# Loading k and v for two pairs of sequences at a time, 1 MB per transfer

## The chip, the cores and the metric

The kernel runs on one core of one Trainium2 chip. The metric is the device time of one execution in microseconds (us). Runs are called fast, or slow when they lie over 1.5% above the fastest run of the same kernel; on one core that label says nothing about why. Profiled times ("span") are a little shorter than the run's time: the span of 386.6 us belongs to a run of 388.32 us.

## The reference, cut to what matters

For each of 16 sequences of 2048 steps and 256 channels, two running sums are carried from step to step; `k`, `v` and the output are 33.6 MB each.

```python
for t in range(seq_len):
    ww = u + kk;       qq = max(pp, ww)            # output of step t
    output[b, t, :] = (e1 * aa + e2 * vv) / (e1 * bb + e2 + 1e-08)
    ww = pp - w + kk;  qq = max(ww, kk)            # state for step t + 1
    aa = e1 * aa + e2 * vv
    bb = e1 * bb + e2
    pp = qq
```

## The kernel before

Time is cut into a short head of 32 steps and 16 *chunks* of 126 steps. Within a chunk the steps lie on the partitions, so the sums over time are matmuls. A *pair* is four sequences of one chunk (two groups of two); four pairs make a chunk, and one pair is one *iteration* of the loop. The output of a pair is made 11 iterations after its input (`LAG`), because it needs the state of all earlier chunks first. Three things matter here.

**The loads.** Each iteration loads `k` and `v` of the pair three iterations ahead, 512 KB each, into one of four buffers. GpSimd issues them, and it also issues the stores of the output, in program order.

```python
AHEAD = 3
kpool = ctx.enter_context(tc.tile_pool(name="kpool", bufs=AHEAD + 1))   # vpool likewise
...
def load(n):
    kr = kpool.tile([128, 4, Dm], F32, tag="kr", name="kr")
    vr = vpool.tile([128, 4, Dm], F32, tag="vr", name="vr")
    ...
        for t, x in ((kr, k), (vr, v)):
            K(POOL.dma_start(out=t[0:r, :, :],
                           in_=x[4 * p:4 * p + 4, t0:t0 + r, :].rearrange("n t d -> t n d")))
```

**The state.** Once a chunk, its column sums `ts` leave the chip's PSUM by ScalarE and are sent by SyncE in six small transfers (`tsum`). VectorE and ScalarE make the new state `ab` from them. SyncE then sends `ab` in four 8 KB transfers into rows 126 and 127 of the tiles `ez`, from where the matmul `den` (128 rows: 126 steps and the state) takes it. Two of the four must be there before the first `den` of the chunk can start.

```python
def inject(c):
    ab = small.tile([128, 2, 64], BF16, tag="ab16", name="ab16")
    K(DVE.tensor_mul(ab, AB.pop(c)[:, :, 0, :], st.pop((c, "phi"))))
    for j in range(2):
        for h in range(2):
            K(SP.dma_start(out=EZ[1 + 2 * c + j][TC + h:TC + h + 1, 0:2, :, :].rearrange(...),
                           in_=ab[64 * j:64 * j + 64, h, :]))
```

**The loop.** The order below is the order on each engine. TensorE, VectorE, ScalarE and GpSimd each take their part of it strictly in turn.

```python
for n in range(NP + LAG + 1):
    ...
    if n + AHEAD < NP:
        load(n + AHEAD)
    small_work(n, "first")
    exps(n)                    # ez = exp(X), ScalarE
    sums(n - 1)                # tot, TensorE
    round_k(n + 1)             # km <- kr, VectorE: the first reader of k
    num(qp, 0); den(q); recip(q); mult(qp, 0); num(qp, 1)
    small_work(n, "pool")      # state_chain, inject
    times_v(n)
    mult(qp, 1); store(qp)
    logs(n + 1)                # X, TensorE
    cast_v(n + 1)              # vb <- vr, VectorE: the first reader of v
```

## Time and profile before

| | before |
|---|---|
| median of 3 runs | 385.43 us (382.28 to 395.25) |
| profiled span, mean granted TensorE clock | 386.6 us, 0.925 |
| busy: TensorE, VectorE, ScalarE, GpSimd | 71%, 78%, 73%, 44% |
| from issue to landing, medians: kr, vr, store | 7.7, 8.1, 6.4 us |
| chunk periods, 157 to 323 us | 18.7 and 22.0 to 23.8 us in turn, mean 20.8 |

The prediction below shows the page's lines and reads them.

The starts of the 66 `ez` activations give the length of every iteration. In the steady part of the kernel before (from 157 us on), three of the four iterations of a chunk take 5.2, 3.8 and 5.8 us (once 6.0). Only the fourth, in which `den` waits for the state, varies: 4.0 us in one chunk, 7.2 to 9.1 us in the next. In each, this is about 3 us and the stall of `den`. So the chunk is 14.8 + 3 + stall, and with the mean stall of 38.5 / 13 = 3.0 us this gives the measured 20.8 us.

The page is of a run that is called slow (388.32 against 382.28 us).

### The profile page before, as it was taken

The page shows a single profiled execution, that of the slowest core. Times are in us where ns is not written, and L with a number is a line of the kernel's source. Part 1 is how long each engine was busy: PE and PEld are TensorE (multiplying, and loading weights), DVE is VectorE, ACT ScalarE, POOL GpSimd, SP SyncE. Part 2 cuts the span into 40 slices and gives each one's busy share as a digit, 9 for nine tenths or more (in the row PEclk, how much of TensorE's full clock was granted, in tenths as well). Part 3 has the DMA queues.
Part 4 walks back from the last instruction along what each step waited for, and adds up shares of the span by engine and source line. Part 5 has one row for each costly group of instructions (what it writes and reads, how often), then busy time and mean ns, then how long its engine had stood idle before and what let it go on. Part 6 is the DMA issues. An engine that isn't in the chain of part 4 may idle for free.

```text
span 386.6 us, 4003 instructions
## 1 busy us (share of the span) xinstructions
PE 275.0 (71%) x1033; PEld 138.0 (36%) x1048; DVE 302.2 (78%) x595; ACT 283.4 (73%) x282; POOL 171.5 (44%) x252
## 2 busy tenths in 40 slices
PE   0276667969886883978598858878587939776771
PEld 0143333435443442434254424444343515322220
DVE  2867789898988885899879977899689967956441
ACT  1165577978897784989598976898698939875571
POOL 7663433554645251555455452546355523121221
PEclk9999989898999896999989998999899978987796
DMA  8499995899999897899989997999899999645454
GB/s 204 130 293 339 332 297 137 269 278 331 330 308 353 290 315 282 236 331 333 352 278 315 314 351 260 332 318 345 290 293 343 303 280 254 198 125 150 128 173 148
DMA packets 49718, 105.72 MB, mean 273 GB/s; under 512 B 24096, under 2 KB 25136, under 8 KB 49696
## 3 DMA queue, kind: packets, MB, share of 16 engines
q0 software_dynamic: 29136, 100.65, 79.3%
q1 hardware_dynamic: 19968, 4.30, 6.0%
q10 hardware_dynamic: 592, 0.52, 0.6%
q8 instruction: 8, 0.13, 0.1%
q14 instruction: 14, 0.11, 0.1%
HBM read 68.11 MB, written 33.55 MB: 263 GB/s over the span
## 4 chain that ended last, share of the span: by engine, by line
ACT 27%; DMA 26%; PE 20%; DVE 12%; issue 10%; POOL 2%; SPq 1%; POOLq 0%; ACTq 0%; DVEq 0%
DMA ez<-ab 17%; ACT ez L252 16%; DMA vr<-in_v_dram 9%; PE X L241 8%; ACT rd L402 5%; PE den L394 5%; PE num L412 4%; PE tot L299 3%; DVE rd L420 3%; ACT ts L309 2%; ACT ts L308 2%; DVE ez L268 2%; DVE vb L260 1%; ACT rd L403 1%; SPq L382 1%
## 5 line engine op out<-in xcount | busy, mean ns | idle before, releaser
L252 ACT ACTIVATE ez<-X 128x2048 bf16<-128x2048 f32 x66 | 122.1, 1850 | 24.8 <-PE X L241 24.7
L436 POOL DMA_DIRECT2D out_dram<-rd x64 | 55.6, 869 | 177.9 <-ACT rd L403 99.7
L420 DVE TENSOR_TENSOR rd<-num,rd 126x512 f32<-126x512 f32 (+1 forms) x131 | 89.8, 685 | 32.2 <-PE num L412 26.9
L268 DVE TENSOR_TENSOR ez<-ez,vb 126x2048 bf16<-126x2048 bf16 (+1 forms) x66 | 80.1, 1213 | 21.6 <-ACT ez L252 20.1
L402 ACT ACTIVATE rd<-den 126x1024 f32<-126x1024 f32 (+1 forms) x66 | 66.7, 1011 | 35.9 <-PE den L394 35.9
L403 ACT ACTIVATE rd<-rd 126x1024 f32<-126x1024 f32 (+1 forms) x66 | 69.4, 1051 | 2.1
L241 PE MATMUL X<-km,NLE 128*128 128x512 f32 x128 | 54.6, 510 | 20.0 <-ACT ez L252 16.6
L412 PE MATMUL num<-ez,LfN 128*128 128x512 bf16 x128 | 51.8, 405 | 23.3 <-DVE rd L420 22.5
L394 PE MATMUL den<-ez,Lf 128*128 128x512 bf16 x113 | 37.6, 404 | 38.5 <-DMA ez<-ab 38.5
L105 POOL DMA_DIRECT2D vr<-in_v_dram x64 | 49.9, 779 | 21.2 <-DVE vb L260 14.9
L105 POOL DMA_DIRECT2D kr<-in_k_dram x64 | 54.4, 851 | 1.4 <-DVE km L233 0.9
L412 PE MATMUL num<-ez,IdN 126*128 126x512 bf16 (+1 forms) x131 | 53.2, 406 | 0.0
L299 PE MATMUL tot<-ez,OHV 126*96 126x512 bf16 x128 | 50.2, 392 | 2.2 <-DVE ez L268 2.2
L299 PE MATMUL tot<-ez,OHE 128*96 128x512 bf16 x128 | 49.7, 388 | 1.1 <-ACT ez L252 1.0
L233 DVE CAST km<-kr 126x1024 fp32r<-126x1024 f32 (+1 forms) x66 | 46.5, 705 | 1.9 <-DMA kr<-in_k_dram 1.6
L260 DVE CAST vb<-vr 126x1024 bf16<-126x1024 f32 (+1 forms) x66 | 45.3, 687 | 0.0
L394 PE MATMUL den<-ez,Id 126*128 126x512 bf16 (+1 forms) x131 | 43.7, 417 | 2.0 <-issue 1.6
L241 PE MATMUL X<-km,NLZ 128*128 128x512 f32 x128 | 41.6, 407 | 0.0
L241 PEld LDWEIGHTS X<-km,NLE 128*128 128x128 f32 x128 | 24.3, 208 | 41.8 <-ACT ez L252 35.3
L394 PEld LDWEIGHTS <-Lf 128*128 128x128 bf16 x128 | 12.1, 101 | 58.2 <-DMA ez<-ab 32.5
L412 PEld LDWEIGHTS <-IdN 126*128 126x128 bf16 (+1 forms) x131 | 13.3, 102 | 51.4 <-issue 44.6
L339 ACT ACTIVATE g<-ex 128x256 f32<-128x256 f32 (+1 forms) x17 | 6.9, 408 | 29.2 <-DVE ex L332 26.9
(89 smaller groups left out, 213.4 us busy)
## 6 DMA issues: line engine op xcount, KB each, us to landing
out_dram<-rd POOLq DMA_DIRECT2D x64, 504.0 KB, 6.4
kr<-in_k_dram POOLq DMA_DIRECT2D x60, 512.0 KB, 7.7
vr<-in_v_dram POOLq DMA_DIRECT2D x60, 512.0 KB, 8.1
tsum<-ts SPq DMA_DIRECT2D x99, 32.0 KB, 5.9
kr<-in_k_dram POOLq DMA_DIRECT2D x4, 504.0 KB, 9.6
vr<-in_v_dram POOLq DMA_DIRECT2D x4, 504.0 KB, 10.9
ez<-ab SPq DMA_DIRECT2D x64, 8.0 KB, 6.9
kr<-in_k_dram SPq DMA_DIRECT2D x3, 128.0 KB, 3.7
```

The costliest lines, as they stand in the source:

```text
L105: K(POOL.dma_start(out=t[0:r, :, :], in_=x[4 * p:4 * p + 4, t0:t0 + r, :].rearrange("n t d -> t n d")))
L241: K(PE.matmul(X[:, q, i, :], m[0:kr, :], km[0:kr, i, :], start=True, stop=True))
L252: K(SC.activation(ez_of(n)[:, 0:4:2], X_of.pop(n)[:, :, 0:i, :], ACT.Exp))
L260: K(DVE.tensor_copy(vb[0:r, 0:i, :], vr_of.pop(n)[0:r, 0:i, :]))
L268: K(DVE.tensor_mul(ez[0:r, 1:4:2], ez[0:r, 0:4:2], vb[0:r, 0:i, :].unsqueeze(1).broadcast_to([r, 2, i, D])))
L299: K(PE.matmul(TOT[c], m[0:r, :], ez_of(n)[0:r, q, i, :], start=n == first_of(c) and i == 0 and q == 0, stop=n == last_of(c) and i == tiles ...
L394: K(PE.matmul(d[:, i, :], m[0:r, :], ez_of(n)[0:r, q, i, :], start=q == 0, stop=q == 2, skip_group_check=True))
L402: K(SC.activation(rd[0:r, 0:i, :], DEN.pop(n)[0:r, 0:i, :], ACT.Ln, scale=RS))
L403: K(SC.activation(rd[0:r, 0:i, :], rd[0:r, 0:i, :], ACT.Exp, scale=-1.0))
L412: K(PE.matmul(d, m[0:r, :], ez_of(n)[0:r, q, i, :], start=q == 1, stop=q == 3, skip_group_check=True))
L420: K(DVE.tensor_mul(RD[n][0:r, i, :], NUM.pop((n, i))[0:r, :], RD[n][0:r, i, :]))
L436: K(POOL.dma_start(out=out[4 * p:4 * p + 4, t0:t0 + TC, :].rearrange("n t d -> t n d"), in_=o[0:TC, :, :]))
```

## The change

The intent is to have half as many transfers of twice the size. The buffers of `k` and `v` hold two pairs, there are two of them instead of four of one pair (the same memory), and both loads are issued together at the end of every even iteration.

```diff
-    kpool = ctx.enter_context(tc.tile_pool(name="kpool", bufs=AHEAD + 1))
-    vpool = ctx.enter_context(tc.tile_pool(name="vpool", bufs=AHEAD + 1))
+    kpool = ctx.enter_context(tc.tile_pool(name="kpool", bufs=2))
+    vpool = ctx.enter_context(tc.tile_pool(name="vpool", bufs=2))
...
-    def load(n):
-        kr = kpool.tile([128, 4, Dm], F32, tag="kr", name="kr")
-        vr = vpool.tile([128, 4, Dm], F32, tag="vr", name="vr")
+    def load(G):
+        kr = kpool.tile([128, 8, Dm], F32, tag="kr", name="kr")
+        vr = vpool.tile([128, 8, Dm], F32, tag="vr", name="vr")
+        for n in (2 * G, 2 * G + 1):
+            i = 4 * (n % 2)
+            kr_of[n], vr_of[n] = kr[:, i:i + 4, :], vr[:, i:i + 4, :]
...
-                               in_=x[4 * p:4 * p + 4, t0:t0 + r, :].rearrange("n t d -> t n d")))
+                               in_=x[4 * p:4 * p + 8, t0:t0 + r, :].rearrange("n t d -> t n d")))
...
-        if n + AHEAD < NP:
-            load(n + AHEAD)
...
             cast_v(n + 1)
+        if n % 2 == 0 and n + 4 < NP:
+            load(n // 2 + 2)
```

More of the change, by code (lines that the diff above doesn't have):

```diff
@@ L44 @@
     NH = NG * GB
-    AHEAD = 3
     LAG = 11
@@ L83, in head_view @@
         return e - b, x[b:e, 0:T0, :].rearrange("n t d -> t n d")
-    def load(n):
-        kr = kpool.tile([128, 4, Dm], F32, tag="kr", name="kr")
-        vr = vpool.tile([128, 4, Dm], F32, tag="vr", name="vr")
-        kr_of[n], vr_of[n] = kr, vr
-        if is_head(n):
-            if n == 1:
-                K(DVE.memset(kr[64:96, 0:2, :], 0.0))
-                K(DVE.memset(vr[64:96, 0:2, :], 0.0))
-            for t, x, eng in ((kr, k, SP), (vr, v, SC)):
-                for g in range(NG):
-                    b = 6 * g + 4 * n
-                    e = min(b + 2 * tiles_of(n), B)
-                    if b < e:
-                        K(eng.dma_start(out=t[g * GB:(g + 1) * GB, 0:e - b, :],
-                                        in_=x[b:e, 0:T0, :].rearrange("n t d -> t n d")))
-        else:
-            c, p = pairs[n]
+    def load(G):
[4 more added lines that the diff above has]
+            kr_of[n], vr_of[n] = kr[:, i:i + 4, :], vr[:, i:i + 4, :]
+            if is_head(n):
+                if n == 1:
+                    K(DVE.memset(kr[64:96, i:i + 2, :], 0.0))
+                    K(DVE.memset(vr[64:96, i:i + 2, :], 0.0))
+                for t, x, eng in ((kr, k, SP), (vr, v, SC)):
+                    for g in range(NG):
+                        b = 6 * g + 4 * n
+                        e = min(b + 2 * tiles_of(n), B)
+                        if b < e:
+                            K(eng.dma_start(out=t[g * GB:(g + 1) * GB, i:i + e - b, :],
+                                            in_=x[b:e, 0:T0, :].rearrange("n t d -> t n d")))
+        if G:
+            c, p = pairs[2 * G]
             t0 = T0 + c * TC
@@ L113 @@
             tensor=x.tensor, offset=x.offset, ap=[[0, 1], [0, 4], list(x.ap[0])])))
-    for n in range(1, AHEAD):
-        load(n)
+    load(1)
     M1 = consts.tile([128, 128], F32, tag="M1", name="M1")
```

## The prediction

> **What bounds the kernel now.** I read the page first, then the waits, then the windows, then the timeline of GpSimd. Each pair of sequences (66 of them: 2 short head pairs, then 16 chunks of 4 pairs) is one iteration of a software-pipelined loop. No engine is full on the page, but the DMA row is:
>
> ```profile
> PE 275.0 (71%) x1033; PEld 138.0 (36%) x1048; DVE 302.2 (78%) x595; ACT 283.4 (73%) x282; POOL 171.5 (44%) x252
> ...
> DMA  8499995899999897899989997999899999645454
> ...
> q0 software_dynamic: 29136, 100.65, 79.3%
> q1 hardware_dynamic: 19968, 4.30, 6.0%
> ```
>
> The digits are tenths of the 16 DMA engines' time in 40 slices of 9.7 us: 9 from slice 3 to slice 34, with a few dips, then about 5 in the tail, where nothing is loaded. q0 holds the loads of k and v and the stores, q1 the small transfers that SyncE issues (`tsum` and `ez<-ab`). The windows view gives the middle, 100 to 345 us:
>
> ```profile
> core 0: us, PE busy (x) PEld busy (x) DVE busy (x) ACT busy (x) POOL busy (x), PEclk, DMA share, GB/s
> 100.00:345.00 245.00, 187.66 (x732) 96.05 (x742) 206.06 (x387) 198.38 (x200) 111.47 (x134) 0.94 0.93 298
> ```
>
> VectorE works 84% of it, ScalarE 81%, the DMA engines 93%. Yet the loads themselves are in time; what waits for DMA is something else, as the view of waits says:
>
> ```profile
> POOL out_dram L436 <- ACT rd L403: 99.7, 35, 7.7
> ...
> PE den L394 <- DMA ez<-ab: 38.5, 13, 6.2
> ...
> POOL vr L105 <- DVE vb L260: 14.9, 7, 3.1
> ...
> DVE km L233 <- DMA kr<-in_k_dram: 1.6, 3, 0.7
> ```
>
> Columns are total us, times, longest. VectorE waited 1.6 us for k. TensorE stood 38.5 us, 13 times, for `ez<-ab`, an 8 KB transfer (four per chunk) that carries the running state into the `den` matmul; it is also the largest item of the chain that ended last (17%). In the timeline those four leave SyncE from 181.06 us on, the first two, which `den` needs, landed at 190.8 and 191.4, and `den` had stood 4.3 us by then. In an idle machine the same transfer is quick: from 345 us on its median is 2.8 us to landing, from 60 to 345 us it is
>
> ```profile
> DMA to landing us min/median/max: 2.1/7.5/10.6
> ```
>
> The landing records show why. A small transfer lands right behind the bulk transfer issued before it: `tsum` issued at 26.35 us landed at 32.79, the load of k issued at 24.05 landed at 32.58. So its latency is the backlog of q0. Latency of `ez<-ab` is a measure of how far the DMA engines are behind, and the stall is how the DMA limit shows itself.
>
> Starts of successive `ts` activations give the chunk periods: 18.7, 22.0, 18.7, 22.9, 18.7, 22.6, 18.7, 23.8 us from 157 to 323 us, mean 20.8. In the 18.7 us chunks the stall is about 1 us and costs nothing (the four iterations take 5.2, 3.8, 5.8 and 4.0 us); in the others it is 4.3 to 5.7 us. So 18.7 us is the pace of the engines without the stall. The DMA's own need per chunk: 8 loads of 512 KB and 4 stores of 504 KB are 1,528 packets of 4 KB. In full stretches the trace has 85 to 90 of them a microsecond, so 17.0 to 18.0 us; `tsum` and `ez` traffic adds about 1 us. That is 18.0 to 19.0 us, level with 18.7. The rest, 20.8 - 18.7 = 2.1 us a chunk, is lost where the queue has nearly run dry and starts again: at 110 to 115, 131 to 135, 154 to 159, 195 to 199 us, once a chunk, packets fall to 40 to 60 a microsecond. It comes after a gap in which GpSimd, whose queue is in order, waits with a store and holds the loads behind it back:
>
> ```profile
> 186.91 0.84 POOL L436 DMA_DIRECT2D out_dram<-rd  x1 [1.35 <-ACT rd L403]
> 187.74 1.14 POOL L105 DMA_DIRECT2D kr<-in_k_dram  x1
> 188.87 0.75 POOL L105 DMA_DIRECT2D vr<-in_v_dram  x1
> 195.19 0.84 POOL L436 DMA_DIRECT2D out_dram<-rd  x1 [5.57 <-ACT rd L403]
> ```
>
> **What the Trainium skill says.** "DMA: Bandwidth & Descriptors", section "Measured (HBM→SBUF, 128 partitions, SWDGE, issued from GpSimd)", advises batching to 1 MiB or more, with 341 GB/s at 1 MB, and the section "Anatomy of one DMA" fits 2.0 us plus bytes over 436 GB/s. That is the reason for this change. The trace agrees on the fixed part where a transfer is alone (a 504 KB store of the tail takes 3.9 to 4.3 us), but not that it is paid each time: with three or more in flight, the loads of 35 to 43 us land every 1.5 us, 512 KB in 1.5 us being 350 GB/s already. The same page, "Issuing engines are not separate DMA queues", says that all queues share 16 engines; the landings above agree. Its section "Queues, rings and completion order" says an engine goes round robin between queues by packets, which would let an 8 KB transfer pass a 1 MB one; the landings above show no such passing. "Trainium Kernel Development and Optimization", "Best Practices", asks for double buffering; two buffers of two pairs are still that.
>
> **The change part by part.** *Removed:* 64 GpSimd issues. 128 loads of about 0.8 us become 64 of perhaps 1.0 us (an estimate: one-row transfers of four pieces took 0.52 us, 128-row ones 0.75, so size counts little). That frees some 40 us of GpSimd, which is 44% busy: off the path, worth 0. *Fixed cost of 64 transfers:* hidden, worth 0. *Bytes and packets:* the same; I expect no better rate, since a row is still pieces of 1 KB in HBM and steady load packets take a constant 192 ns. *SBUF:* 4 buffers of 4 KB a row become 2 of 8 KB, no change.
>
> *Moved:* this is all that is left. Before, loads for pair n+3 follow each iteration's store. Now the loads of pairs n+4 and n+5 follow the store of each even iteration n. The first of the two leaves when it did, the second one iteration earlier, about 5 us; both land only when 1 MB is in. Per chunk q0 gets 2.5 MB, 0.5, 2.5, 0.5 rather than four times 1.5.
>
> Are they in time? From issue to the cast of k there are two iterations, at the shortest 3.8 + 5.8 = 9.6 us, and a little more. With 1.4 us for the store in front, 2.9 us for 1 MB, 2 us fixed, and up to 2 us backlog: 8.3 us. For v, 11.2 us against about 14. In time by 1 to 3 us: 0.
>
> The load that matters is the one before the long gap. `den` of a chunk's first pair, number 4c+2, runs 11 iterations later, in n = 4c+13. That is odd, so the even iteration just before it has queued 2.5 MB instead of 1.5: 1 MB, 2.9 us of work, for the gap in which the queue ran dry. Against it, `ez<-ab` leaves at the end of n = 4c+10, also even, so 2.5 MB go just before it. But the iteration before brought only 0.5, so the two together are the same 3.0 MB; its landing should be some 7.5 to 9 us after issue, where the alternate chunks had 10.
>
> So I expect the alternation of 18.7 and 22.6 to shrink and the chunk to go from 20.8 to about 20.2 us: of the 2.1 us lost to refilling, 1.1 to 1.7 might be won where it works, and I count on it in not quite half of the chunks: 0.6. Over 14 chunks that are at this pace, 8 us. Start-up: pair 3 now loads at 4.6 us rather than 14.4, but pairs 4 and 5 only after the cast of pair 1 at 20.5; k of pair 4 is due at 27.5, estimated to land by 25: 0. Tail (42 us, no loads): 0. Sum: 385.4 - 8 = about 378 us.
>
> **The rivals.** (1) *Nothing*: bytes fix the time. For it: 93% DMA share, unchanged bytes, a near-tie of 3.0 MB before `ez<-ab`. Against it: DMA need is 18 to 19 us of 20.8. Time 383 to 387. (2) *The burst delays the state*: where the queue never ran dry, `ez<-ab` stands behind 1 MB more than before, 2.9 us; if it hits every chunk, +2 us by 14, so about 400 to 410. For it: the in-order landings. Against it: a longer stall drains the queue and so corrects itself. (3) *Empty odd iterations*: the queue runs dry twice a chunk and pays the slow restart twice, +1 us a chunk, about 395. Against it: 3.1 MB fill 9 of the 9.4 us. (4) *Full success*: chunks at 19 us, 14 x 1.8 = 25 us off, 360. For it: the balance of 18.7 and 18 to 19. Against: it leaves no slack anywhere.
>
> **Range and chances.** Centre 378, between rival 1 and rival 4, with the tail of rival 2 and 3 above. The three runs of before alone span 13 us. Range 365 to 392. Faster by over 2% means below 377.7: 0.45. Within 2%: 0.44. Slower: 0.11.
>
> **What would show it.** Right: kr and vr land 8 to 12 us after issue, yet waits of km and vb for DMA stay under 10 us; the wait of `den` for `ez<-ab` falls from 38.5 to 20 to 30 us; DMA share of 100 to 345 us stays at 0.93 or more, with more GB/s than 298; periods nearer 20 with less alternation; GpSimd busy falls below 150 us. Wrong: `ez<-ab` over 10 us in each chunk (rival 2), DMA digits of 7 or 8 in the middle (rival 3), VectorE waiting for kr or vr in tens of us, or load packets at another rate than 192 ns, which would overturn the step that says that size changes nothing.

## The result, and the profile after

The changed kernel took 406.46 us (median of 4 runs, 403.45 to 408.03), the kernel before 385.04 us in the runs beside it. The ratio is 1.0572, with a 95% interval from 1.0477 to 1.0667: slower. Ratios here are the mean time of one kernel's fast runs over that of the other's fast runs of the same rounds, so not quite the ratio of the medians.

| | before | after |
|---|---|---|
| profiled span, mean clock | 386.6 us, 0.925 | 401.6 us, 0.898 |
| landing, medians: kr, vr | 7.7, 8.1 us | 10.1, 11.9 us |
| `den` waits for `ez<-ab` | 38.5 us in 13 | 57.1 us in 13 |
| `km` waits for `kr` | 1.6 us in 3 | 19.5 us in 11 |
| mean chunk period, eight chunks from about 160 us | 20.8 us | 22.3 us |
| from first `ts` to last `ts` | 315.0 us | 334.5 us |

The chunks cost 19.5 us more. The stretch after the last `ts` is 3.9 us shorter than before (45.9 and 42.0 us), which I did not pursue; with 0.6 us won at the start, that makes the 15.0 us between the two spans.

The page of the kernel after, beside the lines of before that the prediction shows:

```profile
PE 280.8 (70%) x1048; PEld 143.2 (36%) x1048; DVE 301.8 (75%) x595; ACT 284.6 (71%) x282; POOL 127.3 (32%) x188
...
DMA  8389977898998969799987989798989999846454
...
q0 software_dynamic: 28112, 100.64, 76.6%
...
kr<-in_k_dram POOLq DMA_DIRECT2D x30, 1024.0 KB, 10.1
vr<-in_v_dram POOLq DMA_DIRECT2D x30, 1024.0 KB, 11.9
```

The busy times of VectorE and ScalarE have hardly changed, so there is no new work. GpSimd has 44 us less. The DMA digits of the middle hold more 7s and 8s than before, and a 6. The last two lines give the time from issue to landing in us. The middle, 100 to 345 us, in the windows view (columns as in the prediction):

```profile
100.00:345.00 245.00, 186.12 (x703) 96.65 (x703) 194.98 (x361) 187.86 (x188) 79.38 (x88) 0.88 0.91 289
```

In the same 245 us VectorE does 11 us and ScalarE 10.5 us less than before, since the loop advances more slowly; the DMA engines fall from 298 to 289 GB/s. The view of waits of the kernel after (total us, times, longest):

```profile
POOL out_dram L436 <- DVE vb L260: 87.1, 23, 8.2
PE den L394 <- DMA ez<-ab: 57.1, 13, 6.6
...
DVE km L233 <- DMA kr<-in_k_dram: 19.5, 11, 4.1
...
DVE vb L260 <- DMA vr<-in_v_dram: 0.3, 1, 0.3
```

Two waits for DMA have changed. That of `den` is 18.6 us longer, and that of `km` for `k`, once next to nothing, is now 19.5 us. The two lie partly beside each other, so they must not be added. The landing of the state's transfers, 60 to 345 us, where before had 2.1, 7.5 and 10.6:

```profile
DMA to landing us min/median/max: 5.7/8.6/11.5
```

What counts is the pair of rows that `den` needs first. Before, from the issue of the first `ez<-ab` of a chunk until both had landed, it was 7.7 to 8.2 us and 10.0 to 11.4 us in turn (157 to 310 us); now it is 9.0 to 12.7 us in every chunk from 78 to 322 us. The mean over the same twelve chunks (the second to the thirteenth) went from 9.3 to 10.5 us. What comes before it (from the first `tsum` to the first `ez<-ab`) has stayed: 4.75 and 4.79 us. The 1.2 us more per chunk are most of the growth of the mean stall, 3.0 us before and 57.1 / 13 = 4.4 us now; the period agrees with that stall, 14.8 + 3 + 4.4 = 22.2 us. The three other iterations still take 5.2, 3.8 and 5.8 us in almost every chunk.

Why do the rows land later? The timeline of GpSimd in one chunk of the kernel after (start, length, what; idle before it in brackets):

```profile
195.19 0.82 POOL L436 DMA_DIRECT2D out_dram<-rd  x1 [2.84 <-ACT rd L403]
196.01 0.93 POOL L106 DMA_DIRECT2D kr<-in_k_dram  x1
196.93 0.90 POOL L106 DMA_DIRECT2D vr<-in_v_dram  x1
206.49 0.85 POOL L436 DMA_DIRECT2D out_dram<-rd  x1 [8.66 <-ACT y L362]
211.34 0.93 POOL L436 DMA_DIRECT2D out_dram<-rd  x1 [4.01 <-ACT rd L402]
212.26 0.93 POOL L106 DMA_DIRECT2D kr<-in_k_dram  x1
213.19 0.90 POOL L106 DMA_DIRECT2D vr<-in_v_dram  x1
```

The 2.5 MB issued at 195 to 198 us had landed by 209.5 us. In the 13.5 us between 197.8 and 211.3 us only one store (504 KB) was issued: the iteration between is an odd one and loads nothing. So the DMA engines run dry, as the windows view of the kernel after shows in its last two columns (DMA share, GB/s):

```profile
206.00:208.00 2.00, 2.00 (x9) 1.00 (x8) 1.59 (x4) 1.75 (x3) 0.85 (x1) 0.79 0.62 217
208.00:210.00 2.00, 2.00 (x11) 1.17 (x10) 1.90 (x3) 1.95 (x5) 0.00 (x0) 1.00 0.75 240
210.00:212.00 2.00, 2.00 (x11) 1.00 (x10) 2.00 (x5) 1.97 (x3) 0.66 (x1) 1.00 0.30 51
212.00:214.00 2.00, 1.43 (x6) 0.53 (x5) 0.93 (x2) 2.00 (x2) 2.00 (x3) 1.00 0.65 146
214.00:216.00 2.00, 2.00 (x10) 1.17 (x10) 2.00 (x3) 1.97 (x3) 0.09 (x1) 1.00 0.78 188
```

They fall to 51 GB/s and need until about 216 us to be back. It is not this chunk alone: counted by microsecond, the packets of loads and stores also fall to between 0 and 29 at 165 to 167, 188, 233 to 234 and 255 to 257 us, each time just before the bunch with which the state leaves. The weakest windows of the kernel before around its store of 195.19 us were these:

```profile
194.00:196.00 2.00, 2.00 (x8) 1.23 (x7) 1.77 (x5) 1.78 (x4) 0.81 (x1) 0.67 0.79 299
196.00:198.00 2.00, 2.00 (x11) 0.96 (x9) 1.59 (x4) 1.98 (x3) 1.59 (x3) 1.00 0.75 203
198.00:200.00 2.00, 2.00 (x10) 1.25 (x9) 2.00 (x3) 1.94 (x4) 0.00 (x0) 1.00 0.94 240
```

Then, at 212.26 us, 2.5 MB come at once, and the state leaves right behind them, at 213.23 us. The chain that ended last shows what it cost (start, length, what; kernel after, 192 to 216 us):

```profile
192.76 9.24 DMA ez<-ab
...
202.14 1.86 PE den L394 x4
...
204.85 1.72 PE X L241 x4
...
213.72 1.22 PE X L241 x4
...
215.57 8.65 DMA ez<-ab
```

The chain runs through the small transfer for 9.2 us in one chunk and 8.7 us in the next. That is its time from issue to landing; TensorE itself stood 6.6 and 4.1 us for them. There is also an aftermath: `X` takes 1.72 us here and 1.22 us a few iterations later, because after 6.6 us of idleness the granted clock was 0.50 from 202 to 206 us. The Trainium skill, "TensorE: Matmul & The Clock Gate", section "Part 1: The HAM clock gate (the "warmup" mystery)", describes this: the array is throttled by default, and some microseconds of activity release it. The trace agrees, and so the lower mean clock of the kernel after (0.898) reads as a consequence of its stalls and not as their cause (before has the same 0.50 at 192 to 194 us, after its stall). It is small: the fourth iteration less its stall is about 3 us in both kernels, 2.7 to 3.4 before and 2.3 to 3.4 after.

To compare kernels by how often the queue ran dry, I counted in each trace the microseconds, of the 250 from 70 to 320 us, in which fewer than 25 packets of loads and stores (those of 4 KB) began. At full rate 85 to 98 begin. Before had 6 such microseconds, after 23. I call them empty microseconds below. The bound of 25 is a choice; with 40 it is 13 and 35.

### The profile page after: what moved, and what is told of

The parts are those of the page before. It is cut to its first block, busy times and chain, and to the rows that moved or that the text cites. A ratio compares the mean times of both kernels' runs of the same rounds, so it can differ in the third digit from the quotient of the medians.

```text
span 401.6 us, 3960 instructions
## 1 busy us (share of the span) xinstructions
PE 280.8 (70%) x1048; PEld 143.2 (36%) x1048; DVE 301.8 (75%) x595; ACT 284.6 (71%) x282; POOL 127.3 (32%) x188
## 4 chain that ended last, share of the span: by engine, by line
DMA 33%; PE 25%; ACT 20%; DVE 9%; issue 8%; POOL 2%; SPq 1%; POOLq 0%; ACTq 0%; DVEq 0%
DMA ez<-ab 22%; PE X L241 10%; ACT ez L252 10%; DMA kr<-in_k_dram 9%; PE den L394 7%; PE num L412 5%; ACT rd L402 4%; DVE rd L420 3%; PE tot L299 3%; ACT rd L403 2%; DMA out_dram<-rd 2%; ACT ts L309 1%; ACT ts L308 1%; DVE ez L268 1%; SPq L382 1%
## 5 line engine op out<-in xcount | busy, mean ns | idle before, releaser
L394 PE MATMUL den<-ez,Lf 128*128 128x512 bf16 x128 | 42.3, 414 | 58.0 <-DMA ez<-ab 57.1
L241 PE MATMUL X<-km,NLE 128*128 128x512 f32 x128 | 58.8, 545 | 15.8 <-ACT ez L252 15.8
L412 PE MATMUL num<-ez,LfN 128*128 128x512 bf16 x128 | 50.9, 398 | 20.4 <-DVE rd L420 19.5
L233 DVE CAST km<-kr 126x1024 fp32r<-126x1024 f32 (+1 forms) x66 | 46.3, 702 | 19.6 <-DMA kr<-in_k_dram 19.5
L299 PE MATMUL tot<-ez,OHE 128*96 128x512 bf16 x128 | 52.3, 408 | 1.1 <-ACT ez L252 1.0
L241 PE MATMUL X<-km,NLZ 128*128 128x512 f32 x128 | 44.9, 435 | 0.0
L241 PEld LDWEIGHTS X<-km,NLE 128*128 128x128 f32 x128 | 26.5, 222 | 35.9 <-ACT ez L252 27.5
L106 POOL DMA_DIRECT2D kr<-in_k_dram x32 | 30.4, 951 | 22.6 <-DVE km L233 22.4
L106 POOL DMA_DIRECT2D vr<-in_v_dram x32 | 29.2, 913 | 10.7 <-DVE vb L260 7.8
L241 PEld LDWEIGHTS X<-km,NLZ 128*128 128x128 f32 x128 | 27.7, 216 | 7.2
## 6 DMA issues: line engine op xcount, KB each, us to landing
kr<-in_k_dram POOLq DMA_DIRECT2D x30, 1024.0 KB, 10.1
vr<-in_v_dram POOLq DMA_DIRECT2D x30, 1024.0 KB, 11.9
kr<-in_k_dram POOLq DMA_DIRECT2D x2, 1008.0 KB, 14.4
```

The costliest lines, as they stand in the source:

```text
L106: K(POOL.dma_start(out=t[0:r, :, :], in_=x[4 * p:4 * p + 8, t0:t0 + r, :].rearrange("n t d -> t n d")))
L233: K(DVE.tensor_copy(KM[n][0:r, 0:i, :], kr_of.pop(n)[0:r, 0:i, :]))
L241: K(PE.matmul(X[:, q, i, :], m[0:kr, :], km[0:kr, i, :], start=True, stop=True))
L299: K(PE.matmul(TOT[c], m[0:r, :], ez_of(n)[0:r, q, i, :], start=n == first_of(c) and i == 0 and q == 0, stop=n == last_of(c) and i == tiles ...
L394: K(PE.matmul(d[:, i, :], m[0:r, :], ez_of(n)[0:r, q, i, :], start=q == 0, stop=q == 2, skip_group_check=True))
L412: K(PE.matmul(d, m[0:r, :], ez_of(n)[0:r, q, i, :], start=q == 1, stop=q == 3, skip_group_check=True))
```

## The experiments

The theory at the outset was that bunching the loads does the harm. With the loads of two iterations issued at once, the queue is first dry and then full, and the state's small transfers land late behind the bunch. The first form of it held that the whole loss passes through the wait of `den` for the state. The rivals: the size of 1 MB itself, since a pair is usable only when two have landed; the new tiles with only two buffers; the place of the bunch just before the state is sent; and the late `k`. Each was timed with the kernel before in the same rounds, whose medians were 380.20, 380.61 and 382.76 us in the three groups of runs, each on another chip. The first group is the next three experiments and the one with the state sent earlier. Comments in the code cuts below are added, and lines are left out.

### One megabyte cut in two halves, in the same place

```diff
-            for t, x in ((kr, k), (vr, v)):
-                K(POOL.dma_start(out=t[0:r, :, :],
-                               in_=x[4 * p:4 * p + 8, t0:t0 + r, :].rearrange("n t d -> t n d")))
+            for i in (0, 4):
+                for t, x in ((kr, k), (vr, v)):
+                    K(POOL.dma_start(out=t[0:r, i:i + 4, :],
+                                   in_=x[4 * p + i:4 * p + i + 4, t0:t0 + r, :].rearrange("n t d -> t n d")))
```

> The changed kernel with each 1 MB load cut into two of 512 KB, issued in the same place (all four after the store of the even iteration). Theory A (place: 2 MB of loads in one bunch stand ahead of the state transfer and leave no loads for the gap after the stall): as slow as the changed kernel, 400 to 411 us, TensorE waiting 50 us or more for ez<-ab, ez<-ab median to landing 8 us or more. Theory B (size: a 1 MB transfer lands as a whole, so k comes late): back to 383 to 391 us, and the wait of km for k gone (under 4 us).

Measured: 398.89 us, ratio 1.0536 (1.0457 to 1.0614), just under the range of theory A.

```profile
PE den L395 <- DMA ez<-ab: 46.9, 13, 5.5
```

The kernel is changed and each transfer is 512 KB as before, and most of the loss remains: `den` waits 46.9 us, `km` only 0.3 us, and there are 20 empty microseconds. So size is not the main cause. What the cut gives back is the wait of `km`, since half of the bunch is usable earlier; for the time that is worth at most a few us.

### The new tiles, but one pair loaded after each iteration

```diff
+    def part(G, i):                       # 512 KB of k and of v, half of a tile
+        ...
-        if n + AHEAD < NP:
-            load(n + AHEAD)
+        if n % 2 == 0 and n + 4 < NP:
+            load(n // 2 + 2)              # first half only
+        if n % 2 == 1 and n + 3 < NP:
+            part(n // 2 + 2, 4)           # second half
```

> The tiles of two pairs stay, but the loads are 512 KB and one pair is loaded after each iteration, as in the kernel before. Theory A and theory B: 381 to 391 us, TensorE waiting 30 to 45 us for ez<-ab. Theory C (the tiles of two pairs with two buffers, whose release is coarser, cost the time): 400 to 410 us.

Measured: 381.76 us, ratio 1.0049 (0.9936 to 1.0163): as before.

```profile
PE den L403 <- DMA ez<-ab: 37.2, 14, 4.5
```

There are 2 empty microseconds. Two tiles of two pairs cost nothing, so long as each iteration brings its own megabyte. This kernel and the one above have the same tiles and the same transfers of 512 KB, and differ only in when the second pair is issued: that is the bunching, and it is worth 17 us.

### The old tiles and sizes, bunched after odd iterations

```diff
+        if n % 2 == 1:
+            for m in (n + 4, n + 5):
+                if m < NP:
+                    load(m)
```

(and the load at the head of the loop removed, pairs 3 and 4 loaded before the loop)

> Tiles and transfers of the kernel before (512 KB, four buffers), but two pairs in a bunch, after odd iterations, so that no bunch stands just ahead of the state transfer (which leaves in an even one) and one follows right after the stall. Theory A in its narrow form (it is the place beside the state transfer): 374 to 390 us, ez<-ab median under 7.5 us, TensorE waiting under 35 us for it. Theory A in its wide form (any bunch of two pairs empties the queue between bunches): 398 to 410 us.

Measured: 401.46 us, ratio 1.064 (1.0516 to 1.0763), 17 empty microseconds. The state is now sent at another place relative to the bunch, yet the loss is the same. The periods show how: 18.9 us in some chunks and 23 to 27 us in the others. `den` waits 48.5 us in 12 stalls, the longest of 8.7 us. A bunch in every second iteration costs as much at this place too, so its place just before the state is not the point. (It is not shown that any bunch does harm: the kernel with held loads, below, issues two pairs at once in one iteration of four, and is fast.)

### The state sent earlier in the iteration

```diff
-                     (s + 5, "exp", inject_weights), (s + 5, "pool", inject)]
+                     (s + 5, "exp", inject_weights), (s + 5, "sums", inject)]
```

> The changed kernel with the state's last product and its four transfers ez<-ab moved up in program order, ahead of the six tsum transfers on SyncE (which take about 4 us to issue), so that they are issued before the bunch of loads. Nothing of the loads is changed. Theory A: ez<-ab lands in 3 to 7 us, TensorE waits under 15 us for it, 370 to 388 us. Theory D (the bound is the emptied queue and late k, and the stall only fills time that is lost anyway): 398 us or more.

Measured: 424.39 us, ratio 1.1232 (1.1123 to 1.1342). The expectation missed. The view of waits of this kernel shows that the aim was reached and that the time went elsewhere:

```profile
PE num L412 <- DVE rd L420: 56.4, 39, 5.1
...
DVE tb L352 <- DMA tsum<-ts: 40.2, 14, 4.8
```

`den` no longer waits for `ez<-ab`, which lands in 2.9 us. But the six `tsum`, the first part of the same round trip, are now behind the bunch (9.5 us to landing), and VectorE stands 40.2 us for them. The edit also did something that I had not meant: it moved `ab` ahead of other work in VectorE's order, where it waits for `phi` (1.6 us in all, so little). And it put `tsum`, the next chunk's first step, behind the `ez<-ab` on SyncE. So its time proves little. What it does show is that a small transfer sent in front of the bunch was fast here, and that the next one behind it paid instead.

### k after even iterations, v after odd ones, 1 MB each

```diff
+            part(G, 0)                     # k of both pairs, even iterations
...
+        if n % 2 == 1 and n + 3 < NP:
+            part(n // 2 + 2, 1)            # v of both pairs, odd iterations
```

> 1 MB transfers, two buffers of two pairs each, but k of the group goes after the even iteration and v after the odd one, so each iteration again queues 1 MB of loads and 0.5 MB of stores. Theory A (bunching): 379 to 391 us, as the kernel before, stall 30 to 45 us. Theory B (size of a transfer): 398 or more.

Measured: 397.73 us, ratio 1.0393 (1.0221 to 1.0565); the profiled run is a slow one. This keeps 1 MB per transfer and brings the same bytes in each iteration. It did what was meant for the state: `den` waits 21.9 us instead of 57.1, and 4 microseconds are empty. But `v` now has one iteration less of lead, and `vb` waits 19.9 us for it in 13 chunks. The expectation missed, and the run doesn't decide what 1 MB without bunching would cost with enough lead.

### Both kernels without the wait for the state

In these two the matmuls contract only the 126 rows of the chunk, without the state's two rows. The result is wrong (relative error 1.35), and nothing waits for `ez<-ab`. The edit is the same in the kernel before and in the kernel after, and is made in `den` and in `num`:

```diff
-        rl, ri = (NH, NH) if is_head(n) else (128, TC)
+        rl, ri = (NH, NH) if is_head(n) else (TC, TC)
```

> The kernel before, but den and num contract over 126 rows instead of 128, so they leave out the two rows that ez<-ab brings and no longer wait for it (a wrong result on purpose; every transfer is still made, at its place). If the stall is what lengthens the chunk from 18.7 to 20.8 us on average: 14 chunks by 2.1 us, 350 to 368 us. If DMA throughput is the bound and the stall only shows it: 374 to 385 us, with new waits for kr, vr or free rd buffers.

> The same with the changed kernel (wrong result on purpose). Theory A (the whole loss of the change goes through the wait for the state): within 1.5% of e10. Theory D (the emptied queue and k landing late cost time of their own): 8 us or more above e10, with DVE waiting 20 us or more for kr.

Measured: before without the wait 365.68 us, ratio 0.965 (0.9564 to 0.9735); after without it 387.82 us, ratio 1.0201 (1.0138 to 1.0264). The first tells what the wait is worth in the kernel before, 15 us of 380.6. The second is the run that felled my theory in its first form: the wait is gone from both, and the changed kernel is still 387.82 - 365.68 = 22.1 us slower. The waits of the kernel after without the state:

```profile
DVE km L233 <- DMA kr<-in_k_dram: 30.2, 13, 4.0
```

Now it is `k` that comes late, 30.2 us in 13 chunks; before without the wait has 11.1 us. One load of `k` was issued at 203.2 us, needed at about 211.2 us and landed at 213.2 us. There are 11 empty microseconds against 4. So what the bunch makes late is not the state alone but whatever is due next.

### A third buffer for k, with and without the wait for the state

```diff
-    kpool = ctx.enter_context(tc.tile_pool(name="kpool", bufs=2))
+    kpool = ctx.enter_context(tc.tile_pool(name="kpool", bufs=3))
...
-            load(n // 2 + 2)
+            load(n // 2 + 2, n // 2 + 3)   # k now two pairs further ahead than v
```

> The changed kernel with a third buffer of two pairs for k: the bunch after each even iteration is still 2 MB, but its k belongs to the group after the next. If k that lands late costs time of its own beside the state's wait: waits of km for kr under 2 us and 385 to 396 us. If the wait for the state binds and k's lateness lies beside it: km's waits gone too, but 399 to 409 us, TensorE waiting 50 us or more for ez<-ab.

> The same third buffer for k, and no wait for the state as in e11 (wrong result on purpose). If late k was all that was left in e11 (387.8 us) against e10 (365.7 us): 363 to 372 us. If the emptied queue costs DMA throughput whatever is waited for: 378 or more, with new waits, for vr or for buffers.

Measured with the state: 408.36 us, ratio 1.0757 (1.0672 to 1.0842). The wait of `km` is gone, that of `den` is 56.9 us, and the time has not fallen. So in the changed kernel the wait of 19.5 us for `k` lies beside the state's wait and costs nothing by itself.

Measured without the state's wait (wrong, as above): 379.39 us, ratio 1.0016 (0.9953 to 1.0079). Of the 22.1 us that remained above, the late `k` was therefore 387.82 - 379.39 = 8.4 us; this compares runs of two groups, on two chips, whose runs of before differed by 2 us. The other 13.7 us, with the same reserve, are still a loss against before without its wait. The trace has these waits for DMA left:

```profile
DVE tb L367 <- DMA tsum<-ts: 17.6, 8, 6.1
...
DVE vb L275 <- DMA vr<-in_v_dram: 6.3, 8, 2.3
```

They are again transfers behind the bunch. That these two make up all of the 13.7 us is argued, not shown.

### Loads held back where the state is sent

If a dry queue and a bunch at the wrong time are the harm, the opposite should help. Here the kernel before gets a fifth buffer, issues no load in the iteration after the one that sends the state, and catches up one iteration later.

```diff
-    AHEAD = 3
+    AHEAD = 4
...
-        if n + AHEAD < NP:
-            load(n + AHEAD)
+        for m in {3: (), 0: (n + AHEAD - 1, n + AHEAD)}.get(n % 4 if n >= 7 else 1, (n + AHEAD,)):
+            if m < NP:
+                load(m)
```

> The kernel before with five buffers of one pair, and in the iteration in which the state is sent no load is issued; the next one loads two pairs. If what delays the state is the bulk queued between tsum and the end of ez<-ab: ez<-ab median 4 to 7 us, stall under 15 us, 358 to 376 us. If total DMA work is the bound: 380 or more.

> e13 again, with more rounds for an interval: 363 to 374 us, ratio to the kernel before 0.955 to 0.98; ez<-ab median 5 to 6 us, all chunks 18.9 us.

Measured: 371.89 us (363.0 to 373.45) against 380.61 us for the kernel before; again, in five rounds, 373.37 us (364.6 to 375.86) against 382.76 us. The runs split into two groups, near 364 and near 373 us, and those of the larger are called slow beside the best, so no ratio is given. In both groups of rounds, every run of this kernel is below every run of the kernel before, and it is right. In the run of 363.0 us the state's needed rows land in 6.3 us instead of 9.3 (means of the same twelve chunks as above), and all chunks from the fourth to the fifteenth take 18.9 us:

```profile
PEld L394 <- DMA ez<-ab: 14.3, 12, 1.9
...
PE den L394 <- DMA ez<-ab: 7.4, 10, 1.2
```

In the run of 373.8 us they take 18.9 us too, except the last, of 27.7 us: a single stall of 9.6 us at 303 us is most of the 10.8 us between the two runs. It falls where the loads of the last chunk are moving (281.6 to 309.9 us): their packets are slower there, a mean of 228 ns against 181 ns in the 20 us before. But in the run of 363.0 us it is much the same (224 against 182 ns) without such a stall, so I have no run that tells why it comes in some executions only.

This kernel also issues two pairs at once, in the iteration that catches up, and has few empty microseconds (7, none between 83 and 310 us). So a bunch once in four iterations, away from the state and with a fifth buffer, did not cost what the bunch in every second one did. Which of these three differences saves it was not tested.

### The fifth buffer alone

```diff
-    AHEAD = 3
+    AHEAD = 4
```

> The control for e13: five buffers of one pair, one pair loaded after each iteration, nothing held. If holding the loads is what gained: 376 to 388 us, as the kernel before. If the fifth buffer gained: 363 to 374 us.

Measured: 383.39 us, ratio 1.0096 (1.0042 to 1.0151), with `den` waiting 37.2 us as before. Loading earlier is worth nothing by itself; the gain of the experiment above is from when the loads are issued.

The counts side by side. Four kernels bunch in every second iteration and keep the state's wait and its place in the order: they have 17 to 23 empty microseconds and take 399 to 408 us.

| kernel | empty microseconds | median, us |
|---|---|---|
| before; one pair each; fifth buffer | 6; 2; 4 | 385; 382; 383 |
| loads held, two runs | 7; 7 | 372; 373 |
| after; halves; bunched odd; third k buffer | 23; 20; 17; 20 | 406; 399; 401; 408 |
| k even, v odd | 4 | 398 |
| no state wait: before; after; after with third k | 4; 11; 5 | 366; 388; 379 |
| state sent earlier | 34 | 424 |

The last three rows, and the held loads, are a warning: the count goes with the time only where nothing else has been moved.

## Why the prediction was wrong

The prediction said 378 us and gave a chance of 0.11 to a slower kernel; measured were 406.46 us.

**What bounds the kernel before: right in the main.** It said that without the stall a chunk takes 18.7 us. Over the same eight chunks, before without the wait for the state took 18.7 to 19.6 us, mean 19.2, and the kernel with held loads 18.9 us. One reading was off. The packets do not fall "once a chunk" to 40 to 60 a microsecond: from 157 us on they fall in every second chunk (195 to 199, 236 to 241, 277 to 282 us), just after the long stall, and at 154 to 155, 237 and 278 to 279 us to 4 to 17. So the dry queue follows the stall: with the wait taken out, 1.6 of the 2.1 us a chunk are won.

**GpSimd's issues: right.** It expected the issue of a 1 MB load to take about 1.0 us and GpSimd's busy time to fall below 150 us. The issues took 0.95 and 0.91 us, and the busy time fell to 127.3 us. It called this worth nothing, and it was.

**Bytes, packets and the fixed cost of 64 transfers: right.** The packets of loads are still 4 KB. From 35 to 43 us, where before moves little but loads, they take 192 ns (median) in both kernels; that is no constant of the whole run, since in the middle, 100 to 345 us, loads and stores together have medians of 165 and 167 ns. Larger transfers brought no better rate, so the very reason for the change had no gain in it. One comparison was loose: the fit that the prediction cites gives 3.2 us for a 504 KB store (an estimate from that page), and the stores of the tail took 3.9 to 4.3 us, so the fixed part from issue to landing is here nearer 3 us than 2.

**k and v in time: the size was off.** The term "In time by 1 to 3 us: 0" rested on 8.3 us for `k` and 11.2 us for `v`, and on "up to 2 us backlog". Measured were 10.1 and 11.9 us. `v` was just in time (0.3 us of waiting); `k` was late in 11 cases, 19.5 us in all. The experiment with a third buffer shows that this cost nothing so long as the state was later still. It was not a step that made the loss, but it takes a share of it once the state's wait is removed (8.4 us).

**The state's landing: this step failed.** The prediction held that `ez<-ab` stands behind the same 3.0 MB and "its landing should be some 7.5 to 9 us after issue, where the alternate chunks had 10". The needed pair took 9.0 to 12.7 us in the twelve chunks counted above. It counted the bytes issued in front and forgot when they were issued. Before, the megabytes of two iterations come some 4 to 6 us apart, and the first has been worked on when the second arrives. After, 2.5 MB of the 3.0 come within 3 us, right in front of the state, and, in the chunks looked at, to a queue that has just been dry and is slow to start. The good chunks of before, 7.7 to 8.2 us, are no longer there.

**The empty odd iteration: this step failed first.** Rival 3 was set aside with "3.1 MB fill 9 of the 9.4 us". That is the work of two average iterations, taken as if it were spread over them. But the bunch of 2.5 MB in the chunk shown had landed after some 14 us (195.2 to 209.5 us), and where the stall makes the iteration long, the next comes 16 us after the one before (196.0 and 212.3 us). The trace has 23 empty microseconds instead of 6, and more DMA digits of 7 and 8, which the prediction itself had named as the sign of rival 3. The queue runs dry once in every chunk, not twice as rival 3 had it. Likewise its own objection to rival 2, that "a longer stall drains the queue and so corrects itself", did not hold: the mean stall grew from 3.0 to 4.4 us. That the drained queue is lost work, and makes the next bunch later, is how I read it; no run separates the two.

So rival 2 was right, and rival 3 in kind. Rival 2 had said +2 us by chunk where it hits every chunk, with 400 to 410 us in all; measured were 1.2 us more for the rows, 1.4 us more of stall and 406.46 us. That the loss comes from issuing the loads of two iterations together, and not from the size, the tiles or the place just before the state, is shown by the three experiments at 398.89, 381.76 and 401.46 us. How it divides between the late state and the dry queue is not: without the wait for the state 22.1 us of difference remain.

**"1 MB more before the long gap": this step failed.** The gain of 8 us rested on it. The long gap of before did get more work, but the other half of the loop was left without any. No period of 18.7 us is left after the change (the shortest of the eight from 164 us on is 20.3 us), where every second chunk had it before.

**"No such passing": only partly right.** The prediction read the small transfers as landing strictly in order. Then what is issued after the state could not matter. The experiment with held loads says that it does: there the loads behind the state are taken away, and the needed rows land in 6.3 us instead of 9.3 (with the fifth buffer alone 8.9). And in the kernel bunched after odd iterations an `ez<-ab` issued at 184.88 us landed at 197.16 us, after a store that was issued later, at 186.78 us, and landed at 194.15 us.

What stays open: why the queue needs some 4 us to be back at full rate after it has run dry; how the 13.7 us without the state and without late `k` are made up; what transfers of 1 MB cost when they are not bunched and have enough lead; and the two groups of times of the kernel with held loads.

## What to carry to other kernels

When DMA is nearly the bound, do not ask only how many bytes are moved and how large each transfer is, but when each is issued: here loads that came two iterations at a time left the queue dry once a chunk and cost 21 us in 385, and whatever was due next behind the bunch landed late. Look for the smallest transfer on the path that closes the loop, read its time from issue to landing chunk by chunk, and keep the large transfers away from it in both directions. Merging transfers gave nothing here, where three and more were in flight and 512 KB already landed every 1.5 us.

## What the Trainium skill lacked or had wrong

- "DMA: Bandwidth & Descriptors", "Measured (HBM→SBUF, 128 partitions, SWDGE, issued from GpSimd)": its advice to batch to 1 MiB or more did not hold here, where three and more transfers are in flight. 512 KB transfers landed every 1.5 us, which is 350 GB/s; with 1 MB the packets from 35 to 43 us took the same 192 ns, and the mean rate of the middle fell from 298 to 289 GB/s through the gaps.
- The same page, "Queues, rings and completion order": it speaks of round robin by packets and of the order of completion, but gives no figure for what a small transfer pays behind a full queue: 8 KB took 2.8 us to landing in the tail, a median of 7.5 us (before) and 8.6 us (after) next to the loads.
- No page that I read says that a queue which has run dry is slow to start: after the gap at 210 to 213 us, 54, 50, 36 and 57 packets began in the next four microseconds, where a full stretch has 85 to 98. The first packets after the gap also take longer, a mean of 238, 242 and 282 ns in the three microseconds from 213 us, where the median of the middle is 167 ns.
- None says that loads of 126 rows (504 KB) land later than those of 128 rows (512 KB): `kr` 9.6 against 7.7 us before, and 14.4 against 10.1 us after with twice the size. While they move, the packets of loads and stores take a mean of 232 and 249 ns, against 193 and 191 ns in the 20 us before. There are only 4 and 2 of them, all in the last chunk, and stores of 126 rows elsewhere show nothing of the kind (6.4 us), so other causes are not ruled out.
